# Gate and up products as 2x2 blocks, with seven block products for three of eight k-tile pairs, in a two-layer encoder trunk on one Trainium2 core

## The chip, the cores and the metric

The kernel runs on one core of one Trainium2 chip. The metric is the device time of one execution in microseconds; the times are medians of several runs. The profile is one further execution with the hardware profiler on.

A core has engines that work side by side, each with its own instruction stream: TensorE (PE in the profile, its weight loads PEld), VectorE (DVE), ScalarE (ACT), GpSimd (POOL) and SyncE (SP), which here starts the weight transfers. TensorE multiplies a stationary tile with a moving one and adds into PSUM; the other engines work from SBUF or PSUM to either.

## What is computed

```python
for layer in range(DEPTH):                       # DEPTH = 2
    h = rms_norm(x, ln_mix_g[layer])             # x: 256 tokens x 2048
    mix = even_mixer(h, ...) if layer % 2 == 0 else odd_mixer(h, ...)
    x = x + mix
    h = rms_norm(x, ln_ffn_g[layer])
    x = x + (jax.nn.silu(h @ wg) * (h @ wu)) @ wd   # wg, wu: 2048 x 5632, wd: 5632 x 2048
```

All of it is float32. Layer 0 mixes by retention and a gated spatial unit, layer 1 by a gated linear recurrence and sparse attention. The change touches the products h @ wg and h @ wu of both layers.

## The kernel before

A product in float32 is made of three matmuls: the weight and the activation are each split into a rounded part hi and a rest lo, and hi x hi, hi x lo and lo x hi are added in PSUM (lines 137 to 139 in `gemm`). The activation is stationary, 128 features by 128 tokens; the weight is the moving operand, 128 features by 512 columns. 256 tokens make two token halves, `th` 0 and 1.

Weights come by SyncE in loads of four k tiles (128 x 2048 floats, 1 MB) into `raw`, of which there are three buffers. `piece` splits 1024 columns of it: ScalarE casts to `hi` (line 93), VectorE subtracts to get `lo` (line 94); four buffers each. So a weight load feeds 24 matmuls of 512 columns.

`ffn` goes through 11 column groups of 512 hidden columns in each layer, in phases of 4, 4 and 3. For a group, the gate product goes over 16 k tiles into two PSUM banks `pg`, ScalarE takes Silu of both halves (line 259), the up product goes into two banks `pu`, and VectorE multiplies (line 263). `to_mix2` then transposes the two halves by TensorE into `pt_hid` and splits them into `hid` (lines 184, 185); it is put into the list `late`, which `gemm` empties after the first weight load of the next product. After each phase the four `pd` products multiply the phase's hidden tiles by wd and VectorE adds them to x (line 239). In the last phase `norm.feed` transposes x for the next norm's operands, `A` (lines 188, 189), `norm.finish` works out each token's factor.

PSUM has eight banks: four carry the tag "mm" (the products of `gemm`), four the tag "sm" (transposes and small products). SBUF temporaries come from one pool `temps` of 17 buffers for the whole kernel.

The order of the instructions on each engine is not the order of the code: a scheduler sets it when the program is built, by its own estimates, and each engine then works strictly in that order, waiting where an operand or a buffer isn't ready. The preparations of layer 1 (masks, a bias table `skew` made by one small product `pbias`, copied to `bt` and written to device memory by GpSimd's queue, line 448) stand in the code before the first FFN.

## Time and profile before

| | |
|---|---|
| median of 3 runs | 2262.45 us (2262.1 to 2263.41) |
| span of the profiled execution | 2260.8 us |
| TensorE busy | 2246.2 us, 99% |
| VectorE busy | 1257.9 us, 56% |
| ScalarE busy | 1013.3 us, 45% |
| device memory read | 414.29 MB, 185 GB/s over the span |
| granted TensorE clock | 0.998 |

The profiled execution's own time is its span, 2260.8 us; the median of the runs without the profiler is 1.65 us above it. A duration in the trace is that of one instruction; two that follow each other may overlap, so the distance of their starts tells more of an engine's pace than their durations. For TensorE above all the pace is read from starts: a product of 512 columns shows 0.39 us, but the next one starts long before that is over.

### The profile page before, as it was taken

The numbers are of one execution on the slowest core, as the hardware profiler recorded it, in microseconds if no ns is written. First come the engines' busy times: TensorE is split into PE (matmuls) and PEld (weight loads), VectorE is DVE, ScalarE is ACT, GpSimd is POOL, SyncE is SP. The second block draws the span as 40 slices with busy tenths as digits, with TensorE's granted clock in tenths as the row PEclk, the third lists the DMA queues.
The fourth block names the chain that finished last, engine by engine and source line by source line (L and its number), as shares of the span: only waits on it lengthen the run. The fifth ranks groups of instructions, "written<-read, shape, count | busy, mean of one in ns | idle before, by whom it ended". The sixth has DMA issues, their size and how long they took to land.

```text
span 2260.8 us, 26089 instructions
## 1 busy us (share of the span) xinstructions
PE 2246.2 (99%) x10397; PEld 1870.2 (83%) x10397; DVE 1257.9 (56%) x1763; ACT 1013.3 (45%) x1268; POOL 12.1 (1%) x24
## 2 busy tenths in 40 slices
PE   9999999999999999999999999999999999999999
PEld 7888888788888888888898888888888888888887
DVE  6645666444544455455555787865445444544554
ACT  6444445344434443444555355554443344434442
POOL 0000000000000000000000000000000000000000
PEclk9999999999999999999999999999999999999999
DMA  8555455655555555555455443355555555555553
GB/s 323 205 187 188 166 179 180 183 186 193 195 189 188 193 195 186 189 196 188 161 196 190 146 149 126 125 188 189 188 196 187 188 191 198 186 188 198 192 186 149
DMA packets 63433, 419.64 MB, mean 186 GB/s; under 512 B 7672, under 2 KB 7672, under 8 KB 15696
## 3 DMA queue, kind: packets, MB, share of 16 engines
q1 hardware_dynamic: 60704, 412.51, 51.0%
q0 software_dynamic: 1312, 3.33, 0.8%
q10 hardware_dynamic: 1296, 2.15, 0.3%
q8 instruction: 81, 1.33, 0.2%
q14 instruction: 40, 0.33, 0.0%
HBM read 414.29 MB, written 3.67 MB: 185 GB/s over the span
## 4 chain that ended last, share of the span: by engine, by line
PE 97%; DMA 1%; DVE 1%; ACT 1%; issue 0%; SPq 0%; ACTq 0%
PE pu L138 8%; PE pu L139 8%; PE pu L137 8%; PE pg L137 7%; PE pg L139 7%; PE pg L138 7%; PE pd L139 7%; PE pd L137 7%; PE pd L138 7%; PE po L139 2%; PE po L138 2%; PE po L137 2%; PE pqk L139 1%; PE pqk L138 1%; PE pqk L137 1%; PE plv L655 1%
## 5 line engine op out<-in xcount | busy, mean ns | idle before, releaser
L94 DVE TENSOR_TENSOR lo<-raw,hi 128x1024 fp32r<-128x1024 f32 (+3 forms) x784 | 948.6, 1211 | 958.2 <-ACT hi L93 957.7
L93 ACT CAST hi<-raw 128x1024 fp32r<-128x1024 f32 (+3 forms) x784 | 817.0, 1043 | 1143.0 <-PE pu L139 300.4
L137 PE MATMUL pu<-hi,A 128*128 128x512 f32 x768 | 300.4, 391 | 4.8 <-ACT hi L93 4.8
L137 PE MATMUL pg<-hi,A 128*128 128x512 f32 x768 | 300.6, 391 | 0.0
L138 PE MATMUL pu<-lo,A 128*128 128x512 f32 x768 | 299.9, 390 | 0.5 <-DVE lo L94 0.5
L139 PE MATMUL pu<-hi,A 128*128 128x512 f32 x768 | 299.8, 390 | 0.0
L139 PE MATMUL pg<-hi,A 128*128 128x512 f32 x768 | 299.0, 389 | 0.0
L138 PE MATMUL pg<-lo,A 128*128 128x512 f32 x768 | 298.8, 389 | 0.0
L137 PE MATMUL pd<-hi,hid 128*128 128x512 f32 x704 | 274.7, 390 | 0.0
L139 PE MATMUL pd<-hi,hid 128*128 128x512 f32 x704 | 274.0, 389 | 0.0
L138 PE MATMUL pd<-lo,hid 128*128 128x512 f32 x704 | 273.9, 389 | 0.0
L137 PEld LDWEIGHTS pu<-hi,A 128*128 128x128 f32 x768 | 144.8, 189 | 35.2 <-ACT hi L93 5.2
L138 PEld LDWEIGHTS pu<-lo,A 128*128 128x128 f32 x768 | 144.8, 189 | 31.1 <-DVE lo L94 1.0
L139 PEld LDWEIGHTS pu<-hi,A 128*128 128x128 f32 x768 | 144.7, 188 | 30.2
L139 PEld LDWEIGHTS pg<-hi,A 128*128 128x128 f32 x768 | 144.2, 188 | 30.1
L137 PEld LDWEIGHTS pg<-hi,A 128*128 128x128 f32 x768 | 144.2, 188 | 29.9 <-issue 0.6
L138 PEld LDWEIGHTS pg<-lo,A 128*128 128x128 f32 x768 | 144.2, 188 | 29.4
L139 PEld LDWEIGHTS pd<-hi,hid 128*128 128x128 f32 x704 | 132.1, 188 | 27.5
L138 PEld LDWEIGHTS pd<-lo,hid 128*128 128x128 f32 x704 | 132.2, 188 | 27.1
L137 PEld LDWEIGHTS pd<-hi,hid 128*128 128x128 f32 x704 | 132.2, 188 | 27.2
L137 PE MATMUL pqk<-hi,A 128*128 128x512 f32 x128 | 50.5, 394 | 0.0
L138 PE MATMUL pqk<-lo,A 128*128 128x512 f32 x128 | 49.9, 390 | 0.0
(337 smaller groups left out, 2322.4 us busy)
## 6 DMA issues: line engine op xcount, KB each, us to landing
raw<-in_wg SPq DMA_DIRECT2D x88, 1024.0 KB, 4.8
raw<-in_wu SPq DMA_DIRECT2D x88, 1024.0 KB, 4.8
raw<-in_wd SPq DMA_DIRECT2D x88, 1024.0 KB, 4.8
raw<-in_ev_in SPq DMA_DIRECT2D x44, 1024.0 KB, 4.8
raw<-in_od_in SPq DMA_DIRECT2D x32, 1024.0 KB, 4.8
raw<-in_ev_out SPq DMA_DIRECT2D x16, 1024.0 KB, 4.8
raw<-in_od_out SPq DMA_DIRECT2D x16, 1024.0 KB, 4.7
raw<-in_od_z SPq DMA_DIRECT2D x8, 720.0 KB, 4.1
```

What stands on the lines that cost most here:

```text
L93: nc.scalar.copy(hi[:, :e], raw[:, o : o + e])
L94: nc.vector.tensor_sub(lo[:, :e], raw[:, o : o + e], hi[:, :e].bitcast(F32))
L137: mm(ps[th], xh[:, c], hi[:, j, :], start=i + j == 0, stop=False)
L138: mm(ps[th], xh[:, c], lo[:, j, :], start=False, stop=False)
L139: mm(ps[th], xl[:, c], hi[:, j, :], start=False, stop=i + j == total - 1)
L655: mm(ps[:, i, th, :], lhs[:, i, t], rhs[:, i, t], start=True, stop=True)
```

## The change

Each weight load now holds two k tiles of gate and the same two of up for a column group: gate of the first, gate of the second, up of the second, up of the first (`_gate_up`, in the host's layout). `gate_up` takes the place of the two `gemm` calls of a group. The eight loads of a group are its k-tile pairs 0 to 7. A pair is a product of 2x2 blocks: two token halves by two k tiles, times two k tiles by gate and up.

Pairs 0, 2, 3, 5 and 7 do the eight block products as before, 24 matmuls, into the banks q2 (gate, half 0), q4 (gate, half 1), q3 (up, half 0) and q8 (up, half 1). Pairs 1, 4 and 6 (`MIXED`) do seven: VectorE makes four sums of weight blocks (`sum`), ScalarE and VectorE split three plain blocks (`hu`, `lu`, 1536 columns) and the four sums (`ht`, `lt`, 2048 columns), and each of the seven products goes into one of seven banks: q1, q5, q6 and q7 are of the tag "sm", q2, q3 and q4 are those of the plain pairs. After pair 6, ScalarE copies q1 and VectorE works out u2, u3, v and w from q1, q5, q6 and q7; after pair 7 these are added to q2, q4, q3 and q8, then come Silu and the product. The activation's side of the blocks is made once for each norm, by `left` for the tiles 1, 4 and 6.

The temporaries come from a pool for each stage (`m0`, `f0`, `m1`, `f1`), opened and closed around it. The preparations of layer 1 now stand in the code behind the first FFN, with the pool `m1`. GpSimd's transfer descriptors get 4096 bytes instead of the default. Comment lines are emptied.

```diff
+MIXED = (1, 4, 6)
...
+    def stage(name, bufs):
+        stack = ExitStack()
+        now["T"] = stack.enter_context(tc.tile_pool(name="T" + name, bufs=bufs))
+        return stack
...
+    def left(src, gs):
+        g, h = T([4, 128], "g"), T([4, 128], "h")
+        nc.scalar.activation(g[:, 0:4:3, :], src[:, 0, :].rearrange("p (i n) -> p i n", i=2), AF.Copy, scale=gs[0])
+        nc.scalar.activation(g[:, 1:3, :], src[:, 1, :].rearrange("p (i n) -> p i n", i=2), AF.Copy, scale=gs[1])
+        nc.vector.tensor_sub(h[:, 0, :], g[:, 3, :], g[:, 2, :])
+        nc.vector.tensor_sub(h[:, 3, :], g[:, 0, :], g[:, 3, :])
+        nc.vector.tensor_sub(h[:, 1, :], h[:, 0, :], g[:, 0, :])
+        nc.vector.tensor_add(h[:, 2, :], g[:, 1, :], h[:, 1, :])
+        out = []
+        for t, n in ((g, 3), (h, 4)):
+            a = act.tile([128, 2, 4, 128], F32R, tag="A", name="A", bufs=8 + len(MIXED))
+            nc.scalar.copy(a[:, 0, 0:n, :], t[:, 0:n, :])
+            nc.vector.tensor_sub(a[:, 1, 0:n, :], t[:, 0:n, :], a[:, 0, 0:n, :].bitcast(F32))
+            out += [(a[:, 0, i, :], a[:, 1, i, :]) for i in range(n)]
+        return out
...
+    def gate_up(w, n, fp):
+        q = {}
+        def bank(i):
+            if i not in q:
+                q[i] = (PS if i in (1, 5, 6, 7) else PM)([512], f"q{i}")
+                return q[i], True
+            return q[i], False
+        def product(i, x2, hi, lo, last=False):
+            (xh, xl), (ps, first) = x2, bank(i)
+            mm(ps, xh, hi, start=first, stop=False)
+            mm(ps, xh, lo, start=False, stop=False)
+            mm(ps, xl, hi, start=False, stop=last)
+        c = {}
+        for j in range(8):
+            raw = load(w[j], 2048)
+            end = j == 7
+            if j not in MIXED:
+                a = n.tiles[j]
+                for o, cols in ((0, ((2, 0), (4, 1))), (1024, ((3, 0), (8, 1)))):
+                    hi, lo = piece(raw, o, 2, 512)
+                    for i, th in cols:
+                        t = slice(128 * th, 128 * th + 128)
+                        for e in range(2):
+                            kt = 1 - e if o else e
+                            product(i, (a[:, kt, 0, t], a[:, kt, 1, t]), hi[:, e, :], lo[:, e, :], end and e == 1)
+            else:
+                a11, a12, a22, d1, d2, d3, d4 = n.tiles[j]
+                r = raw.rearrange("p (i n) -> p i n", i=4)
+                sm = fp.tile([128, 4, 512], F32, tag="sum", name="sum")
+                nc.vector.tensor_add(sm[:, 0:2, :], r[:, 0:3:2, :], r[:, 3:4, :].to_broadcast([128, 2, 512]))
+                nc.vector.tensor_add(sm[:, 2, :], sm[:, 0, :], r[:, 2, :])
+                nc.vector.tensor_add(sm[:, 3, :], sm[:, 2, :], r[:, 1, :])
+                parts = []
+                for src, m, name in ((r[:, 0:3, :], 3, "u"), (sm, 4, "t")):
+                    hi = fp.tile([128, m, 512], F32R, tag="h" + name, name="h" + name)
+                    lo = fp.tile([128, m, 512], F32R, tag="l" + name, name="l" + name)
+                    nc.scalar.copy(hi, src)
+                    nc.vector.tensor_sub(lo, src, hi.bitcast(F32))
+                    parts += [(hi[:, i, :], lo[:, i, :]) for i in range(m)]
+                b11, b21, b22, s1, s2, s3, s4 = parts
+                last = j == MIXED[-1]
+                product(1, a11, *b11, last)
+                product(2, a12, *b21)
+                product(3, d3, *b22)
+                product(5, d1, *s1, last)
+                product(7, d4, *s2, last)
+                product(6, d2, *s3, last)
+                product(4, a22, *s4)
+                if last:
+                    c1 = T([512], "c1")
+                    nc.scalar.copy(c1, q[1])
+                    u2, u3, v, w_ = T([512], "u2"), T([512], "u3"), T([512], "v"), T([512], "w")
+                    nc.vector.tensor_add(u2, c1, q[6])
+                    nc.vector.tensor_add(u3, u2, q[7])
+                    nc.vector.tensor_sub(v, q[5], u2)
+                    nc.vector.tensor_sub(w_, q[5], u3)
+                    c = {2: c1, 4: u3, 3: v, 8: w_}
+            if j == 0:
+                flush()
+            elif j == 1:
+                flush2()
+        for i in (2, 4, 3, 8):
+            nc.vector.tensor_add(c[i], q[i], c[i])
...
     def ffn(layer, n, norm):
+        f = stage(f"f{layer}", TF)
+        fp = f.enter_context(tc.tile_pool(name=f"sums{layer}", bufs=1))
         for g0, gn in ((0, 4), (4, 4), (8, 3)):
             hid = []
             for g in range(g0, g0 + gn):
-                pg = two(512, "pg")
-                gemm(pg, wg[g], n.get, 512, range(4))
...
-                pu = two(512, "pu")
-                gemm(pu, wu[g], n.get, 512, range(4))
...
+                late.append(partial(to_mix2, gate_up(wgu[g], n, fp), "hid", hid))
...
+    ffn(0, nf0, n1)
...
+    c1 = stage("m1", TB)
+    lp = c1.enter_context(tc.tile_pool(name="l1", bufs=1))
     masks = lp.tile([128, 7, 128], I32, name="masks")
```

The scheduler's order shows the new work at three places. First VectorE where one column group ends and the next is under way, before: two products with the up half, `s`, stand between plain splits, and the two splits of hidden tiles follow three plain splits later (`lo` and `hi` are split weights, `pu` a PSUM bank, `r` the tokens' factor).

```order
L94 TENSOR_TENSOR lo_3966<-raw_3963,hi_3965 128x1024
L263 SCALAR_TENSOR_TENSOR s0_3767<-pu0_3771,r_3067,s0_3767 128x512
L263 SCALAR_TENSOR_TENSOR s1_3768<-pu1_3772,r_3067,s1_3768 128x512
L94 TENSOR_TENSOR lo_3982<-raw_3963,hi_3981 128x1024
L94 TENSOR_TENSOR lo_4000<-raw_3997,hi_3999 128x1024
L94 TENSOR_TENSOR lo_4016<-raw_3997,hi_4015 128x1024
L185 TENSOR_TENSOR hid_3947<-pt_hid_3948,hid_3947 128x2x256
L185 TENSOR_TENSOR hid_3955<-pt_hid_3956,hid_3955 128x2x256
```

After, on VectorE at the same place, with the four additions of banks (`c1`, `u3`, `v`, `w`), and `lt`, the 2048-column split of the next group's pair 1.

```order
L350 TENSOR_TENSOR c1_3916<-q2_3657,c1_3916 128x512
L350 TENSOR_TENSOR u3_3919<-q4_3664,u3_3919 128x512
L350 TENSOR_TENSOR v_3920<-q3_3675,v_3920 128x512
L325 TENSOR_TENSOR lt_4033<-sum_4024,ht_4032 128x2048
L350 TENSOR_TENSOR w_3921<-q8_3682,w_3921 128x512
L354 SCALAR_TENSOR_TENSOR c1_3916<-v_3920,r_3069,c1_3916 128x512
L354 SCALAR_TENSOR_TENSOR u3_3919<-w_3921,r_3069,u3_3919 128x512
L104 TENSOR_TENSOR lo_4064<-raw_4061,hi_4063 128x1024
L104 TENSOR_TENSOR lo_4080<-raw_4061,hi_4079 128x1024
L104 TENSOR_TENSOR lo_4098<-raw_4095,hi_4097 128x1024
L195 TENSOR_TENSOR hid_4006<-pt_hid_4007,hid_4006 128x2x256
L195 TENSOR_TENSOR hid_4014<-pt_hid_4015,hid_4014 128x2x256
```

The splits of the hidden tiles still come three plain splits behind the last product, but ahead of these rows there now stand `lt` of pair 6, two plain splits, the three additions and `lu` of the next group's pair 1, and u2, u3, v and w. Second, TensorE behind the transposes of a hidden tile, before: products into `pg`, banks of the other tag.

```order
L178 MATMUL pt_hid_3658<-ident_80,s0_3469 128x128
L178 MATMUL pt_hid_3658<-ident_80,s1_3470 128x128
L137 MATMUL pg0_3613<-hi_3667,A_2802 128x512
L138 MATMUL pg0_3613<-lo_3668,A_2802 128x512
L139 MATMUL pg0_3613<-hi_3667,A_2802 128x512
```

These products wait for no bank that the transposes use. After, the end of the first mixed pair that follows the transposes:

```order
L296 MATMUL q5_4046<-ht_4032,A_2727 128x512
L297 MATMUL q5_4046<-lt_4033,A_2727 128x512
L298 MATMUL q5_4046<-ht_4032,A_2727 128x512
L296 MATMUL q7_4050<-ht_4032,A_2727 128x512
L297 MATMUL q7_4050<-lt_4033,A_2727 128x512
L298 MATMUL q7_4050<-ht_4032,A_2727 128x512
L296 MATMUL q6_4054<-ht_4032,A_2727 128x512
L297 MATMUL q6_4054<-lt_4033,A_2727 128x512
L298 MATMUL q6_4054<-ht_4032,A_2727 128x512
L296 MATMUL q4_3981<-ht_4032,A_2724 128x512
```

Here q7 and q6 take the banks of the two `pt_hid` tiles, and wait for the two hidden splits shown above.

Third, TensorE around the small product behind which the bias table is copied and written, before: between the first mixer's output (`po`) and the first FFN (`pg`).

```order
L138 MATMUL po1_2858<-lo_2936,mixb_2367 128x512
L139 MATMUL po1_2858<-hi_2935,mixb_2367 128x512
L445 MATMUL pbias_2966<-onehot_2961,relb_2963 8x384
L137 MATMUL pg0_2989<-hi_2993,A_2706 128x512
L138 MATMUL pg0_2989<-lo_2994,A_2706 128x512
```

After, between the end of the first FFN (`pd`) and layer 1's first products (`pz`).

```order
L148 MATMUL pd1_8007<-lo_8119,hid_7668 128x512
L149 MATMUL pd1_8007<-hi_8118,hid_7668 128x512
L555 MATMUL pbias_8154<-onehot_8149,relb_8151 8x384
L147 MATMUL pz0_8176<-hi_8180,A_7787 128x360
L148 MATMUL pz0_8176<-lo_8181,A_7787 128x360
```

The copy `bt` and the write of `skew` follow this product, and so move from the first FFN to layer 1's start.

## Rows read from the trace of the kernel before

**Rows 1.** The page's first part (busy us, share, count), then TensorE's waits.

```profile
PE 2246.2 (99%) x10397; PEld 1870.2 (83%) x10397; DVE 1257.9 (56%) x1763; ACT 1013.3 (45%) x1268; POOL 12.1 (1%) x24
...
PE pu L137 <- ACT hi L93: 4.8, 1, 4.8
```

**Rows 2.** Timeline of TensorE, two stretches (start us, us, engine, line, operation).

```profile
443.14 1.03 PE L178 MATMUL pt_hid<-ident,s 128*128 128x128 f32 x8
...
444.48 0.39 PE L139 MATMUL pg<-hi,A 128*128 128x512 f32 x1
...
513.18 0.39 PE L138 MATMUL pu<-lo,A 128*128 128x512 f32 x1
513.41 0.39 PE L139 MATMUL pu<-hi,A 128*128 128x512 f32 x1
...
521.80 0.39 PE L137 MATMUL pu<-hi,A 128*128 128x512 f32 x1
```

**Rows 3.** VectorE's groups by form (busy us, mean ns | idle), then VectorE's timeline.

```profile
L94 DVE TENSOR_TENSOR lo<-raw,hi 128x1024 fp32r<-128x1024 f32 x756 | 924.9, 1224 | 931.8 <-ACT hi L93 931.5
...
L263 DVE SCALAR_TENSOR_TENSOR s<-pu,r,s 128x512 f32<-128x512 f32 x44 | 30.9, 743 | 0.0
L185 DVE TENSOR_TENSOR hid<-pt_hid,hid 128x512 fp32r<-128x512 f32 x44 | 28.2, 682 | 0.0
...
L683 DVE TENSOR_TENSOR qp<-qp,em 128x128 f32<-128x128 f32 x48 | 13.5, 282 | 1.6 <-PE pl L670 1.5
...
L94 DVE TENSOR_TENSOR lo<-raw,hi 128x768 fp32r<-128x768 f32 x4 | 3.8, 958 | 6.9 <-ACT hi L93 6.9
...
L690 DVE TENSOR_TENSOR em<-em 128x128 f32<-128x128 f32 x4 | 1.1, 287 | 0.0
...
15.68 2.35 DVE L94 TENSOR_TENSOR lo<-raw,hi 128x1024 fp32r<-128x1024 f32 x2
...
40.93 0.16 DVE L168 SCALAR_TENSOR_TENSOR nr_y<-nr_t,nr_y 128x2 f32<-128x2 f32 x1
41.12 0.17 DVE L230 COPY r<-nr_y 128x2 f32<-128x2 f32 x1
...
371.71 1.28 DVE L239 TENSOR_TENSOR x<-po,x 128x512 f32<-128x512 f32 x2
```

**Rows 4.** ScalarE's groups by form, then the timeline where engines hand over.

```profile
L93 ACT CAST hi<-raw 128x1024 fp32r<-128x1024 f32 x756 | 796.0, 1053 | 1117.8 <-PE pu L139 300.4 <-PE pd L139 271.2 <-PE pg L139 269.1
...
L184 ACT CAST hid<-pt_hid 128x512 fp32r<-128x512 f32 x44 | 23.5, 586 | 0.0
...
L93 ACT CAST hi<-raw 128x768 fp32r<-128x768 f32 x4 | 3.3, 834 | 5.2 <-PE phq L139 3.8 <-issue 1.5
...
501.85 0.39 PE L139 MATMUL pg<-hi,A 128*128 128x512 f32 x1
...
502.28 1.05 ACT L93 CAST hi<-raw 128x1024 fp32r<-128x1024 f32 x1 [1.67 <-PE pg L139]
...
503.36 1.22 DVE L94 TENSOR_TENSOR lo<-raw,hi 128x1024 fp32r<-128x1024 f32 x1 [1.50 <-ACT hi L93]
```

**Rows 5.** Transfers (KB, us to landing), TensorE's timeline, one window (PEclk third from the end).

```profile
raw<-in_wu SPq DMA_DIRECT2D x88, 1024.0 KB, 4.8
...
raw<-in_od_z SPq DMA_DIRECT2D x8, 720.0 KB, 4.1
...
skew<-bt POOLq DMA_DIRECT2D x1, 1536.0 KB, 34.8
...
raw<-in_wu SPq DMA_DIRECT2D x1, 1024.0 KB, 23.8
...
417.74 0.79 PE L137 MATMUL pu<-hi,A 128*128 128x512 f32 x1 [4.75 <-ACT hi L93]
...
424.28 0.40 PE L138 MATMUL pu<-lo,A 128*128 128x512 f32 x1
...
420.00:425.00 5.00, 5.00 (x15) 3.87 (x14) 3.59 (x3) 4.09 (x5) 0.00 (x0) 0.57 0.59 210
```

More of the change, by code (lines that the diff above doesn't have):

```diff
@@ L70, in trunk @@
     nc.scalar.activation(warm, warm, AF.Gelu)
-    idle = tp.tile([128, 512], F32R, tag="T", name="idle")
+    c0 = stage("m0", TB)
+    idle = T([512], "idle", F32R)
     nc.gpsimd.memset(idle.bitcast(F32), 0.0)
@@ L209, in operand @@
         def operand(self, i, src):
-            a = act.tile([128, 2, 2, S], F32R, tag="A", name="A")
-            split(a, src, [gain(self.g0 + 2 * i), gain(self.g0 + 2 * i + 1)])
+            gs = [gain(self.g0 + 2 * i), gain(self.g0 + 2 * i + 1)]
+            if i in self.mixed:
+                self.tiles.append(left(src, gs))
+                return
+            a = act.tile([128, 2, 2, S], F32R, tag="A", name="A", bufs=8 + len(MIXED))
+            split(a, src, gs)
             self.tiles.append(a)
@@ L248, in out_proj @@
                     late.append(partial(norm.feed, c))
+    def gate_up(w, n, fp):
[61 more added lines that the diff above has]
+            nc.vector.tensor_add(c[i], q[i], c[i])
+        s = []
+        for th, (g, u) in enumerate(((2, 3), (4, 8))):
+            nc.scalar.activation(c[g], c[g], AF.Silu, scale=n.tok(th))
+            nc.vector.scalar_tensor_tensor(c[g], c[u], n.tok(th), c[g], op0=OP.mult, op1=OP.mult)
+            s.append(c[g])
+        return s
@@ new lines, in load_ln @@
+    def load_ln(q):
+        for at, t, src in ((1, lng, "sgu_g"), (4, lnb, "sgu_b")):
+            if q == at:
+                nc.sync.dma_start(t, d[src].rearrange("(o c n) -> o c n", o=1, c=2).to_broadcast([128, 2, 512]))
+    vs = [[None, None], [None, None]]
+    vps = []
+    for c in range(2):
+        ps = two(512, "pvs")
+        gemm(ps, win[10 + c], n0.get, 512, range(4), before=load_x if c else first_norm, quick=c == 0)
+        vps.append(ps)
+    nc.sync.dma_start(wsT, d["sgu_wT"])
@@ new lines, in trunk @@
+    nc.sync.dma_start(rot, d["rot"])
+    nc.sync.dma_start(dm, d["decay"])
+    v, sg = [[None, None], [None, None]], [[None, None], [None, None]]
+    for c in range(2):
+        ps = two(512, "pv")
+        gemm(ps, win[4 + c], n0.get, 512, range(4))
+        for th in range(2):
+            v[th][c] = T([512], "v")
+            nc.scalar.activation(v[th][c], ps[th], AF.Copy, scale=n0.tok(th))
+    for c in range(2):
+        ps = two(512, "pg0")
+        gemm(ps, win[6 + c], n0.get, 512, range(4))
+        for th in range(2):
+            sg[th][c] = T([512], "sg")
+            nc.scalar.activation(sg[th][c], ps[th], AF.Silu, scale=n0.tok(th))
@@ new lines, in trunk, with rotate @@
+    cs = lp.tile([128, 2, 2, 128], F32, name="cs")
+    sc = lp.tile([128, 2, 2, 128], F32, name="sc")
+    for th in range(2):
+        nc.vector.tensor_scalar(cs[:, th], rot[:, th], n0.tok(th), None, op0=OP.mult)
+        for i in range(2):
+            nc.vector.tensor_copy(sc[:, th, i, :], cs[:, th, 1 - i, :])
+    mixb = []
+    def rotate(rr, ts):
+        for i in range(2):
+            pt = turn([r[:, 256 * i : 256 * i + 256] for r in rr], "pqkT")
+            t = T([2, S], "qkT")
+            nc.scalar.copy(t, pt)
+            ts.append(t)
@@ L803, in _wide, with _gate_up @@
     return np.ascontiguousarray(w).reshape(c // n, k // (128 * dk), 128, dk * n)
+def _gate_up(g, u):
+    g, u = (w.reshape(8, 2, 128, -1, 512).transpose(3, 0, 2, 1, 4) for w in (g, u))
+    return np.ascontiguousarray(np.stack([g[:, :, :, 0], g[:, :, :, 1], u[:, :, :, 1], u[:, :, :, 0]], 3)).reshape(-1, 8, 128, 2048)
 def _cols(v):
```

262 lines of the change are left out of this document (109 added, 153 removed).

## The prediction

> **What bounds the kernel now.** I read the busy shares of the page first: the reader is to see that TensorE is busy for 2246.2 of 2260.8 us, while VectorE and ScalarE are busy for 56% and 45% [rows 1]. Then the waits of TensorE: outside the start, the only one of weight is 4.8 us, once, for a split of weights in the first FFN [rows 1]. So almost every microsecond is a product that follows the one before. The timeline of one column group gives their pace: products start at 513.18, 513.41, ... 521.80 us, 38 steps in 8.62 us, 0.2267 us each [rows 2]. The eight transposes of a finished hidden tile and two products take 443.14 to 444.48 us, so the transposes cost 1.34 - 2 x 0.2267 = 0.89 us [rows 2]. A column group of gate and up is 2 x 16 k tiles x 2 token halves x 3 = 192 products: 43.5 us, with its transposes 44.4 us. The kernel has 22 of them, 43% of its time.
>
> **What is taken away.** Five k-tile pairs keep 24 products (120), three have seven block products of three matmuls each (63): 183 instead of 192. The order shows 9584 TensorE rows against 9782: 198 = 22 x 9 fewer. All stood on the path, so 198 x 0.2267 = 44.9 us go, if TensorE stays the bound. The weights moved are the same: eight loads of 1 MB per group.
> The pace is a row, and a page can be set beside it. The Trainium skill, "TensorE: Matmul & The Clock Gate", section "Back-to-back issue gap", gives N / 2.4 + 2.5 ns, about 216 ns for 512 columns: an estimate of 42.7 us by it. The trace shows 227 ns here.
>
> **What VectorE gets instead.** Durations and starting distances are two things. One split of 128x1024 takes 1.224 us, but two that wait for nothing take 2.35 us together, so the second starts 1.13 us after the first; two additions of 128x512 (0.682 us) take 1.28, a distance of 0.60. One that needs the result of the one before starts only after its end: 40.93, then 41.12, for 0.16 us [rows 3]. From 128x768 (0.958) to 128x1024 (1.224) a column costs 1.04 ns, which makes 1.76 us for 1536 and 2.29 us for 2048 columns, distances 1.67 and 2.20 [rows 3]. A mixed pair costs VectorE three additions (1.13 + 0.71 + 0.60) and two splits (1.67 + 2.20): 6.3 us, where TensorE needs 21 x 0.2267 = 4.8 us for it. A group: ten plain splits 11.3, three mixed pairs 19.0, four combinations of banks 2.5, four additions of banks 2.4, two products with the up half 1.3, two splits of hidden tiles 1.2: 37.7 us, against 20.6 before and 42.4 us that TensorE now needs (183 x 0.2267 + 0.89). VectorE is at 89% in these stretches, but still the smaller. No row shows the additions on weights; that they cost what other fp32 additions cost I take from the rows nearest to them, on tiles with strides and a repeated operand, where 128x128 takes 0.282 us against 0.287 without [rows 3]. ScalarE: ten casts of 1.053 [rows 4], three of 1.49 and three of 1.93 (by the same slope, 0.834 to 1.053), one copy, two Silu, two hidden casts: 24 us of 42.4, hidden.
>
> **Where VectorE's order can hold TensorE.** All eight PSUM banks are now in use inside a group: q2, q4, q3, q8 in one set of four, q1, q5, q7, q6 in the other, which the transposes pt_hid share. By the order, q7 and q6 of the first mixed pair of a group wait until the two hidden splits of the group before have read pt_hid. These two stand on VectorE behind a long row: the 2048 columns of the last mixed pair, the preparation of the next group's first mixed pair, the combinations and additions of the banks, and three plain splits. I follow it from E, the end of the products of pair 4. ScalarE sees an end 0.2 us late (501.85 + 0.39, cast at 502.28, minus the 0.227 of a step) and hands on in 0.03 us [rows 4], so its 2048-column cast (1.93) lets VectorE start at E + 2.16. The row up to the hidden splits sums, by distances, to 2.20 + 3 x 1.13 + 0.71 + 0.60 + 1.67 + 0.71 + 6 x 0.60 + 2.20 + 0.60 + 2 x 0.66 + 3 x 1.13 = 20.4: it reaches them at E + 22.6. Their ScalarE casts end at E + 22.9: TensorE comes to the transposes at E + 5.44 + 4.76 + 5.44 + 5.44 = E + 21.08, ScalarE first does a cast that waits for the same point (1.05), then 0.59. So the banks are free at E + 23.6 and E + 24.2; TensorE, undisturbed, begins pair 1 after the transposes, at E + 21.97, and takes q1, q2, q3, q5, q7, q6, q4 in this order, 0.68 us each: it wants q7 at E + 24.7 and q6 at E + 25.4. A margin of 1.1 us: I take this at nothing. It is the narrowest place, and lies at 16 transitions (three, three and two in each layer; after the last group of a phase the down products follow, which need neither). A raw tile adds little: the last mixed pair's buffer is free at the end of its 1536-column split, some 1.4 us before E + 2.16; the next load lands 4.8 us later [rows 5], within 0.1 us of when the next addition wants it (E + 5.5).
>
> **Smaller terms.** The first group of each layer follows a norm: two of the three mixed operands of a layer were built earlier, the third, and the 14 small steps of the norm's factor, 0.19 us apart [rows 3], stand on VectorE between the preparations of pairs 1 and 4. Laid out in the same way, the 2048-column splits come 1.1 and 0.6 us late: 2 us a layer, 4 in all, between 0 and 8.
> The 1.5 MB write of the bias table, skew, moves. Before it runs beside the start of the first FFN: it takes 34.8 us, and a weight load issued beside it 23.8 us instead of 4.8 [rows 5]. TensorE runs dry: 4.75 us idle, then from 417.74 to 424.28 us thirteen products in 6.54 us instead of 2.95, at a granted clock of 0.57 between 420 and 425 us, its lower level of 1.2 GHz for most of that [rows 5]. Together 4.75 + 3.6 = 8.3 us. This goes from the FFN. But the table's tile now comes from the pool of layer 1, opened after the FFN, and the write is issued after the one small product ahead of pz. There loads are 720 KB, 4.1 us each [rows 5], and feed TensorE for some 4 us apiece instead of 5.44, so the same loads in flight cover less. I let the loss return with 3 us on top; bounds are -8.3 (the smaller loads slip through) and +8 (a load comes after 20 us, while the three buffers hold 12 us of work). On GpSimd's queue the same four small loads and two memsets stand ahead of the write as before. For the smaller descriptor area of these transfers no row gives a price; the write is the only large one, and its bounds cover that.
> The pools by stage open where their memory was last used tens of microseconds before; the order shows no engine that waits there for the end of a stage in front of others but the casts above. Nothing, up to 2 us.
>
> **Sum**, against the profiled execution: 2260.8 - 44.9 + 4 + 3 = 2222.9 us; the median of the runs lies 1.65 us above that span, so 2224.5 us.
>
> **Rivals.** *VectorE's row ends last.* If every step waits for the end of the one before, as the dependent ones do (duration + 0.03), the row is 5 x 1.224 + 1.22 + 1.36 + 1.76 + 8 x 0.682 + 2 x 2.29 + 2 x 0.743 + 21 x 0.03 = 22.6 us instead of 20.4: the first hidden split ends at E + 25.5, and TensorE stands 0.8 us for q7. Sixteen times that is 13 us, 2237 us; with late loads on top it may be 1.5 us each, 24 us, 2249 us. It decides once the row is 1.1 us longer. For it: VectorE at 89% and in order. Against: the distances in [rows 3].
> This is also what a rule makes of it: the Trainium skill, "VectorE: DVE Perf Modes", section "Terms", says of the DRAIN after each operation that the "next op can't issue until 8-slice pipe empties". By that rule, full durations add up and 2237 us result; the trace agrees for dependent steps (0.19 us apart at 0.16 us) but not for independent ones, 0.60 apart at 0.68.
> *VectorE becomes the bound, and the kernel slower.* The additions on strided weight tiles (1.13 + 0.71 + 0.60) might run at half pace, 2.1 us more a pair, 6.4 a group: 44.1 us, as long as a group before, so no gain, about 2262; with full durations (37 steps x 0.085 = 3.1) 47.2 us, 22 x 2.8 = 62 us more than before, about 2325. It decides at 44.4 us a group, 2.2 us more for each mixed pair. Against it speak the two 128x128 rows in [rows 3].
> *The write of the table is covered* beside pz: 8.3 + 3 us less, 2213 us. For it the smaller loads, against it the 23.8 us.
>
> **How the numbers follow.** Forecast, 2215 to 2236 us: 0.62. VectorE's row last, 2236 to 2249: 0.20. Table covered and nothing else late, below 2215: 0.07. VectorE's additions dearer, gain eaten up: 0.05 within 0.2% of before and 0.06 slower (0.2% is about what a measurement of this kernel tells from no change). Range 2214 to 2248 us: the forecast, nearly all of the first rival and the edge of the third, 0.82. Faster 0.89, same 0.05, slower 0.06.
>
> **What would show it.** Products 0.2267 us apart inside mixed pairs too; 198 fewer; VectorE near 38 us per column group, 828 us in all 22 instead of 453, its 1024-column addition near 1.22 us. TensorE's waits: if the forecast holds, none for the hidden splits at q7 or q6 in pair 1 but for the first group of a layer; if the first rival, 0.8 us and more at 16 places. No gap near 410 us, one near 1100 to 1140 us beside pz. The prediction is wrong if TensorE waits inside a column group at other places (a 2048-column split of pair 4 or 6 that comes late), or if a product's pace changes with the order of the weights.

## The result, and the profile after

The changed kernel takes 2230.9 us, median of 4 runs (2228.9 to 2232.1), the kernel before 2262.3 (2262.1 to 2263.4): a ratio of 0.986, interval 0.9846 to 0.9874. It is faster by 31.4 us, where the forecast had 38. The profiled execution after spans 2229.0 us, before 2260.8.

The page's first part answers to [rows 1]:

```profile
PE 2211.7 (99%) x10199; PEld 1833.3 (82%) x10199; DVE 1613.1 (72%) x2161; ACT 1107.1 (50%) x1302; POOL 12.1 (1%) x24
```

So do TensorE's waits (engine, line, releaser: total us, times, longest); of weight are:

```profile
PE pz L147 <- ACT hi L103: 7.9, 1, 7.9
...
PE pz L148 <- DVE lo L104: 0.7, 2, 0.4
```

198 products are gone (10397 to 10199), TensorE is still the bound, and no wait stands in a column group. The wait before at L137 in the first FFN is gone, and one beside pz has come. Windows over the first FFN and over pz, of the kernel before (columns: stretch, us, then busy time and count of PE, PEld, DVE, ACT and POOL, granted clock, DMA share, GB/s):

```profile
383.30:1125.00 741.70, 736.48 (x3294) 609.31 (x3293) 374.12 (x364) 315.05 (x343) 1.08 (x1) 1.00 0.54 188
1125.00:1157.20 32.20, 32.20 (x201) 32.17 (x200) 19.07 (x36) 17.61 (x27) 0.00 (x0) 1.00 0.56 192
```

And of the changed kernel: one column group, the first FFN, pz, and five microseconds inside pz:

```profile
458.00:500.84 42.84, 42.84 (x192) 35.17 (x191) 38.19 (x38) 23.21 (x21) 0.00 (x0) 1.00 0.54 197
382.40:1097.80 715.40, 715.40 (x3192) 588.33 (x3190) 552.39 (x567) 361.89 (x357) 3.03 (x5) 1.00 0.53 193
1097.80:1142.40 44.60, 35.98 (x201) 34.96 (x201) 17.95 (x35) 16.50 (x27) 1.10 (x1) 0.89 0.66 173
1120.00:1125.00 5.00, 0.00 (x0) 0.00 (x0) 0.00 (x0) 0.00 (x0) 0.00 (x0) 0.80 0.49 103
```

The first FFN is 26.3 us shorter; pz is 12.4 us longer, and for five whole microseconds of it no engine computes while the DMA engines are half busy: the table's write takes 34.8 us, as in [rows 5]. TensorE's granted clock is 0.89 in pz, against 1.00 before. A column group takes 42.84 us, where 42.4 were reckoned. The difference is in the mixed pairs. TensorE's timeline of plain pair 3 of a group (from 527.90) and of the mixed pair 4 behind it (start us, us, engine, line, operation):

```profile
527.90 0.39 PE L296 MATMUL q<-hi,A 128*128 128x512 f32 x1
...
533.34 0.40 PE L296 MATMUL q<-hu,A 128*128 128x512 f32 x1
...
538.23 0.39 PE L296 MATMUL q<-hi,A 128*128 128x512 f32 x1
```

24 plain products take 5.44 us, 0.2267 each, as in [rows 2]; the 21 of the mixed pair take 4.89, 0.233 each (4.89 or 4.90 in the pairs 4 and 6 of that FFN; 4.97 or 4.98 in pair 1 where it stands behind the transposes). Nothing is waited for there, the granted clock is 1.00, and the first few products of the next plain pair are slow as well (5.46 us for its 24). Found here, this pace was the question for the experiments; the table's write was the other.

VectorE's prices came as reckoned (line, names, shapes, count | busy us, mean ns | idle before):

```profile
L325 DVE TENSOR_TENSOR lt<-sum,ht 128x2048 fp32r<-128x2048 f32 x66 | 151.0, 2287 | 44.9 <-ACT ht L324 44.9
L325 DVE TENSOR_TENSOR lu<-raw,hu 128x1536 fp32r<-128x1536 f32 x66 | 115.7, 1753 | 14.6 <-ACT hu L324 14.6
L317 DVE TENSOR_TENSOR sum<-raw 128x1024 f32<-128x1024 f32 x66 | 80.3, 1217 | 0.0
L319 DVE TENSOR_TENSOR sum<-sum,raw 128x512 f32<-128x512 f32 x66 | 45.5, 690 | 1.8
```

### The profile page after: what moved, and what is told of

Its sections match the earlier page's. It is cut to its first block, busy times and chain, and to the rows that moved or that the text cites. A ratio compares the mean times of both kernels' runs of the same rounds, so it can differ in the third digit from the quotient of the medians.

```text
span 2229.0 us, 26164 instructions
## 1 busy us (share of the span) xinstructions
PE 2211.7 (99%) x10199; PEld 1833.3 (82%) x10199; DVE 1613.1 (72%) x2161; ACT 1107.1 (50%) x1302; POOL 12.1 (1%) x24
## 4 chain that ended last, share of the span: by engine, by line
PE 97%; DMA 1%; DVE 1%; ACT 0%; issue 0%; SPq 0%; ACTq 0%
PE q L296 14%; PE q L297 14%; PE q L298 14%; PE pd L149 7%; PE pd L148 7%; PE pd L147 7%; PE po L149 3%; PE po L148 2%; PE po L147 2%; PE pqk L149 1%; PE pqk L148 1%; PE pqk L147 1%; PE plv L758 1%; DMA raw<-in_od_z 1%; PE pt_hid L188 1%; PE pvs L147 1%
## 5 line engine op out<-in xcount | busy, mean ns | idle before, releaser
L103 ACT CAST hi<-raw 128x1024 fp32r<-128x1024 f32 (+3 forms) x652 | 677.6, 1040 | 936.1 <-PE q L298 277.4
L104 DVE TENSOR_TENSOR lo<-raw,hi 128x1024 fp32r<-128x1024 f32 (+3 forms) x652 | 781.8, 1206 | 492.1 <-ACT hi L103 490.6
L297 PE MATMUL q<-lo,A 128*128 128x512 f32 x880 | 343.1, 390 | 0.0
L296 PE MATMUL q<-hi,A 128*128 128x512 f32 x880 | 343.1, 390 | 0.0
L298 PE MATMUL q<-hi,A 128*128 128x512 f32 x880 | 342.6, 389 | 0.0
L296 PEld LDWEIGHTS q<-hi,A 128*128 128x128 f32 x880 | 165.2, 188 | 35.3
L297 PEld LDWEIGHTS q<-lo,A 128*128 128x128 f32 x880 | 165.2, 188 | 35.3
L298 PEld LDWEIGHTS q<-hi,A 128*128 128x128 f32 x880 | 165.2, 188 | 35.0
L325 DVE TENSOR_TENSOR lt<-sum,ht 128x2048 fp32r<-128x2048 f32 x66 | 151.0, 2287 | 44.9 <-ACT ht L324 44.9
L324 ACT CAST ht<-sum 128x2048 fp32r<-128x2048 f32 x66 | 126.2, 1912 | 59.8 <-PE q L298 51.9
L325 DVE TENSOR_TENSOR lu<-raw,hu 128x1536 fp32r<-128x1536 f32 x66 | 115.7, 1753 | 14.6 <-ACT hu L324 14.6
L298 PE MATMUL q<-ht,A 128*128 128x512 f32 x264 | 104.3, 395 | 0.0
L296 PE MATMUL q<-ht,A 128*128 128x512 f32 x264 | 103.6, 395 | 0.0
L317 DVE TENSOR_TENSOR sum<-raw 128x1024 f32<-128x1024 f32 x66 | 80.3, 1217 | 0.0
```

Source lines behind the costliest of these rows:

```text
L103: nc.scalar.copy(hi[:, :e], raw[:, o : o + e])
L104: nc.vector.tensor_sub(lo[:, :e], raw[:, o : o + e], hi[:, :e].bitcast(F32))
L296: mm(ps, xh, hi, start=first, stop=False)
L297: mm(ps, xh, lo, start=False, stop=False)
L298: mm(ps, xl, hi, start=False, stop=last)
L317: nc.vector.tensor_add(sm[:, 0:2, :], r[:, 0:3:2, :], r[:, 3:4, :].to_broadcast([128, 2, 512]))
```

## The experiments

**Which operand is slow?** p1_operands puts one side of the block products back to the plain kind, in each of the three mixed pairs another; p2_quiet leaves out the sums and splits of nearly all mixed pairs, and with them that work of VectorE and ScalarE beside the products.

p1_operands:

```
+                if j == 4:                       # stationary tiles of plain pair 3
+                    a = n.tiles[3]
+                    sides = [(a[:, i % 2, 0, 128 * (i // 2) : 128 * (i // 2) + 128], ...) for i in range(4)]
+                    a11, a12, a22, d1, d2, d3, d4 = sides + sides[:3]
+                if j == 6:                       # moving tiles of plain pair 5
+                    b11, b21, b22, s1, s2, s3, s4 = [(hi5[:, i % 2, :], lo5[:, i % 2, :]) for i in range(7)]
+                if j == 1:                       # two banks instead of seven
+                    for k, (x2, w2) in enumerate(...):
+                        product((2, 4)[k % 2], x2, *w2)
```

> The changed kernel with one operand of the block products put back to the plain pairs' kind in each of the three mixed pairs, so that its numbers are not the reference's: pair 1 sums its seven products into two banks (q2 and q4 in turn) instead of seven; pair 4 takes its stationary tiles from the plain pair 3 instead of the blocks that left() made; pair 6 takes its moving tiles from the splits of the plain pair 5 instead of hu, lu, ht and lt. The sums and splits still run. In the changed kernel the 21 products of a mixed pair take 4.90 us (pairs 1 and 6) and 4.97 us (pair 4, which the transposes stand ahead of), where 21 of the plain distance 0.2267 us are 4.76 us. If the slower pace comes from the number of banks, pair 1 falls to about 4.76 and the others stay. If it comes from the stationary blocks, pair 4 falls to about 4.83. If it comes from the moving tiles' place or row length, pair 6 falls to 4.76. If it comes from the work of VectorE and ScalarE beside the products, none of them changes.

(The text on record has the transposes ahead of pair 4; they stand ahead of pair 1.) p2_quiet keeps hu to lt of a layer's first mixed pair:

```
+                if kept:
+                    parts = kept[0]
+                else:
+                    ...
+                    kept.append(parts)
```

> The changed kernel with the sums and splits of the mixed pairs made once a layer (in its first column group's first mixed pair) and used by all later mixed pairs, so that its numbers are not the reference's: 65 of 66 times VectorE's 1.22 + 0.68 + 0.69 + 1.75 + 2.29 us and ScalarE's 1.48 + 1.91 us are left out in each layer but for the first pair. Products, their operands' places and their banks stay as they are. If the work of VectorE and ScalarE beside the products slows them, the 21 products of a mixed pair take 4.76 us instead of 4.90, and the span falls by about 9 us to 2220. If it is the operands or the banks, they stay at 4.90 us, and the span stays within 2 us of 2229, since nothing of the sums was waited for.

(The text on record counts 65 of 66 pairs; by the edit it is 32 of the 33 mixed pairs of each layer.)

TensorE's timeline of p1_operands, pair 1 from 517.07, pair 4 from 532.97 and pair 6 from 543.33, which now has plain moving tiles:

```profile
517.07 0.48 PE L296 MATMUL q<-hu,A 128*128 128x512 f32 x1
...
522.04 0.39 PE L296 MATMUL q<-hi,A 128*128 128x512 f32 x1
...
532.97 0.40 PE L296 MATMUL q<-hu,A 128*128 128x512 f32 x1
537.87 0.39 PE L296 MATMUL q<-hi,A 128*128 128x512 f32 x1
...
543.33 0.39 PE L296 MATMUL q<-hi,A 128*128 128x512 f32 x1
...
548.09 0.39 PE L296 MATMUL q<-hi,A 128*128 128x512 f32 x1
```

Pair 4 keeps 4.90 us with other stationary tiles, pair 1 keeps 4.97 with two banks; pair 6 takes 4.76 for its 21 products (2228.0 us in all, one run). So it is something about the moving tiles. In p2_quiet, pair 6:

```profile
543.52 0.40 PE L296 MATMUL q<-hu,A 128*128 128x512 f32 x1
548.41 0.39 PE L296 MATMUL q<-hi,A 128*128 128x512 f32 x1
```

4.89 us still, and 2229.5 us in all (one run): neither the mixed pairs' own work on VectorE and ScalarE nor a wait for it is the cause. The plain splits still run beside the products.

**Place, shape or data?** p3_place sets plain splits high and part of the sums' splits low.

```
+                    if j == 3 and not o:     # four tiles of 512 columns in the stage's pool
+                        hl = [T([512], "tmp", F32R) for _ in range(4)]
+                    elif j == 5 and not o:   # two tiles of 1024 columns behind lt
+                        hf, lf = (fp.tile([128, 2, 512], F32R, tag=t, name=t) for t in ("hf", "lf"))
...
+                    if j == 6 and m == 4:    # the sums' splits in the plain hi and lo
+                        for o in (0, 1024):
+                            hi, lo = piece(s2, o, 2, 512)
```

> The changed kernel, its sums unchanged, with three sets of moving tiles at other places in SBUF, so that the place is told from the tiles' shape and from the data. In the changed kernel the plain pairs' splits lie at 30 to 62 KB of a partition, hu to lt at 187 to 216 KB. Here the first half of pair 3 (plain, 12 products) lies in four tiles of 512 columns at 158 to 179 KB, the first half of pair 5 (plain, 12 products) in two tiles of 1024 columns at 216 to 224 KB, and the second part of pair 6 (12 products of the sums' splits) in the plain pairs' tiles at 30 to 62 KB. If the place makes the moving tiles slow, pair 5 rises from 5.46 to about 5.54 us (12 times 0.0063 us) and pair 6 falls from 4.89 to about 4.81; pair 3 tells whether 158 to 179 KB is slow too (5.44 or 5.52). If it is the 1536 and 2048 columns of their tiles, pair 3 and 5 stay and pair 6 falls. If it is the data (sums and differences), all three stay at 5.44, 5.46 and 4.89.

Its timeline: the first half of pair 5 (hf) and the second part of pair 6 (hi):

```profile
538.79 0.39 PE L296 MATMUL q<-hf,A 128*128 128x512 f32 x1
541.59 0.39 PE L296 MATMUL q<-hi,A 128*128 128x512 f32 x1
...
546.43 0.39 PE L296 MATMUL q<-hi,A 128*128 128x512 f32 x1
549.17 0.39 PE L296 MATMUL q<-hi,A 128*128 128x512 f32 x1
```

Twelve plain products with hf take 2.80 us; twelve block products with hi take 2.74, where twelve times 0.2267 is 2.72 and the first few still lag; the first half of pair 3 took 2.79 instead of 2.72 (2232.6 us in all, one run). So neither data nor the tiles' length counts. I read this as: high in SBUF is slow. It was wrong, because two things had been moved at once: hi and lo begin at a multiple of 1024 bytes, all the tiles high up 640 bytes past one.

**The table's write.** s1_spread and b1_before_spread write it in pieces, in the changed kernel and in the one before.

```
-    nc.gpsimd.dma_start(skew, bt[0:8, None, :].to_broadcast([8, 128, 384]))
...
+                if layer == 0 and g < 8:
+                    nc.scalar.dma_start(skew[g], bt[g : g + 1, None, :].to_broadcast([1, 128, 384]))
```

> The changed kernel with the position bias table written in eight pieces of 192 KB, one head each, from ScalarE's queue at the ends of the first eight column groups of the first FFN, instead of one write of 1536 KB from GpSimd's queue beside the first layer-1 products (pz). If the 12.4 us that pz lost (1157.2 to 1142.4 us for its end against 1125.0 to 1097.8 for its start) are due to that one write, pz goes back to the 32.2 us that it took in the kernel before, and if a piece fits in the slack of the loads (4.8 us to land against 5.4 us of products on a load), the FFN loses nothing: 2230.9 - 12.4 = 2218.5 us. If the pieces hold back the loads as the whole did (8.3 us for 1536 KB in the first FFN of the kernel before), the gain is 12.4 - 8.3 = 4 us: 2227 us. If pz was late for another cause (the wait for the pools of the new stage), it stays at 2231.

> The kernel before with the same table written in the same eight pieces inside the first FFN. There the one write cost 8.3 us, the 68 products that raw loads held back: 2262.3 - 8.3 = 2254 us if the pieces fit in the slack, 2262 if they hold the loads back as the whole did. The difference of this kernel and the changed kernel with the same pieces is then the block products' own gain without the table's write: 44.9 us less what the slower pace in the mixed pairs costs (10.4 us by the profile's start distances) and what the first column groups lose (0 to 4): 31 to 35 us if the pace is the mis-sized term, 41 if the pace's excess is no real time.

Both came out slower than any time that was expected: 2238.4 us (ratio to before 0.9896, 0.9881 to 0.9911) and 2278.4 (1.0075, 1.0059 to 1.0092). The pieces were not where the code has them. Nothing but the table was needed for them, so the scheduler that orders the program put them ahead: in s1_spread they are issued from 286 to 396 us, beside layer 0's last products. The transfers there (KB each, median us to landing):

```profile
skew<-bt ACTq DMA_DIRECT2D x8, 192.0 KB, 8.8
```

Two of the issues in ScalarE's queue:

```profile
315.02 0.49 ACTq L367 DMA_DIRECT2D skew<-bt  x1
...
330.78 0.49 ACTq L367 DMA_DIRECT2D skew<-bt  x1
```

And TensorE behind these two pieces:

```profile
317.97 0.50 PE L148 MATMUL po<-lo,mixa 128*128 128x512 f32 x1 [2.54 <-DVE lo L104]
...
333.85 0.60 PE L148 MATMUL po<-lo,mixa 128*128 128x512 f32 x1 [2.66 <-DVE lo L104]
```

TensorE waits there for 2.5 us and more (until 317.97 and 333.85) for a split of weights, and it would be easy to take this for the price of a piece. The engines that make the split show another cause. ScalarE's cast of these weights and VectorE's row ahead of the first wait:

```profile
306.85 1.05 ACT L103 CAST hi<-raw 128x1024 fp32r<-128x1024 f32 x1 [3.52 <-PE po L149]
...
313.65 0.69 DVE L271 TENSOR_TENSOR x<-po,x 128x512 f32<-128x512 f32 x1 [10.08 <-PE po L149]
...
316.69 1.23 DVE L104 TENSOR_TENSOR lo<-raw,hi 128x1024 fp32r<-128x1024 f32 x1
```

And the same kind of split in the changed kernel:

```profile
312.95 1.23 DVE L104 TENSOR_TENSOR lo<-raw,hi 128x1024 fp32r<-128x1024 f32 x1 [1.50 <-ACT hi L103]
```

The weights had landed and their cast was over at 307.90. But VectorE stands idle for 10.08 us until 313.65: two additions to x, which wait for TensorE's sums, and six small steps of the norm are ahead of the split in its order. In the changed kernel the split follows its cast. Ahead of the second wait, too, VectorE is idle for such an addition (4.32 us, until 329.42) while a cast that was over at 327.27 waits for its split, until 332.58; and in the 5 us behind the issues at 286.10 and 364.64 TensorE waits for nothing. So these waits come from the order that the scheduler chose for the program with the pieces; b1_before_spread has the same row (10.09 us of idle time, the split at 316.59). The loads beside the pieces do land later (7.2 to 8.3 us in the median between 280 and 420 us, instead of 4.8), but what a piece costs by itself is not shown: the two runs did not test it. So instead of placing the write, s2_row and b2_before_row make it small: one row a head, read with a positive step and turned round on VectorE.

```
-    skew = dp.tile([8, 128, 384], F32, name="skew")
+    skew = dp.tile([8, 384], F32, name="skew")
-    nc.gpsimd.dma_start(skew, bt[0:8, None, :].to_broadcast([8, 128, 384]))
+    nc.gpsimd.dma_start(skew, bt[0:8])
-    ... offset=base.offset + 127, ap=[[383, 128], [1, 256]]))
+    ... offset=base.offset + 1, ap=[[1, 128], [1, 256]]))
-                                               bias[:, i, 256 - n : 256], op0=OP.mult, op1=OP.add)
+                                               bias[:, i, 0:n][:, ::-1], op0=OP.mult, op1=OP.add)
-    ... == bucket[None, :]).astype(f))
+    ... == bucket[None, ::-1]).astype(f))
```

> The changed kernel with the bias table written once as 8 rows of 384 (12 KB instead of 1536 KB) at the same place in the program, its columns turned round; the reads take the same 128 KB each, and VectorE reads the tile backwards. If the write's size is what delays pz, the 7.9 us wait goes and pz takes 32.2 us again instead of 44.6: 2230.9 - 12.4 = 2218.5 us, range 2216 to 2222. If pz waits for the pools of the new stage and the small loads behind them, it stays at 2231.

> The kernel before with the same small table at its own place, ahead of the first FFN. The first FFN's 8.3 us of waiting for raw loads goes: 2262.0 - 8.3 = 2253.7 us, range 2251 to 2256, if the write is its cause; 2262 if not. The changed kernel with the small table then stands against it by the block products alone: 44.9 us less 9 to 10 us of slower pace less 0 to 4 us of first groups, 31 to 36 us; the forecast's own terms (44.9 less 4) would give 41.

2218.25 us (0.9807, 0.9792 to 0.9822) and 2253.4 (0.9961, 0.9947 to 0.9975): both within 0.4 us of the main expectation. The transfer in s2_row:

```profile
skew<-bt POOLq DMA_DIRECT2D x1, 12.0 KB, 1.7
```

No wait at pz is left in its trace. The write cost 12.7 us beside pz and 8.9 beside the first FFN.

**Is it the place?** s3_low moves the activations up, so that the block tiles come down to 64 to 121 KB; q1_before_high moves the weights of the kernel before up; p4_step sets the block tiles across the middle.

```
-    act = ctx.enter_context(tc.tile_pool(name="acts", bufs=8))
+    act = ctx.enter_context(tc.tile_pool(name="acts", bufs=8, side="right"))     # s3_low
...
-    wp = ctx.enter_context(tc.tile_pool(name="weights", bufs=4))
+    wp = ctx.enter_context(tc.tile_pool(name="weights", bufs=4, side="right"))   # q1_before_high
...
+    xp = ctx.enter_context(tc.tile_pool(name="xs", bufs=4))                      # p4_step, on s3_low
+        pad = fp.tile([128, PAD], F32, name="pad")                               # PAD = 3400
```

> The changed kernel with the small bias table (12 KB) and one more edit: the pool of the activations (x, the left operands, the hidden tiles) goes to the upper end of SBUF, so that the stage's temporaries and hu, lu, ht and lt lie at 64 to 121 KB of a partition instead of 158 to 216 KB. The plain splits stay at 30 to 62 KB. If it is the place that makes the moving tiles slow, the 21 products of a mixed pair take 4.76 us instead of 4.90 (and the first pair behind them 5.44 instead of 5.46), 10.4 us in 66 pairs: 2218.25 - 10.4 = 2208 us, range 2205 to 2212. If the place does not matter, or 64 to 121 KB is as slow as 158 KB, it stays at 2218.

> The kernel before with the weights' pool at the upper end of SBUF: the raw tiles at 172 to 197 KB and the moving tiles hi and lo at 197 to 229 KB of a partition, instead of 17 to 75 KB; the rest moves down. Nothing else changes. If the place sets the pace, every product of the weights takes 0.2333 us instead of 0.2267: 382 loads of 24 products of 512 columns, 9168 times 0.0066 = 60 us, 2262.3 + 60 = 2322 us. If it is peculiar to the block products, it stays at 2262.

> The changed kernel with the small table and the blocks' tiles set across the middle of SBUF, to find where the slow part begins: hu at 122.8 to 128.9 KB (in thousands of bytes), lu at 128.9 to 135.1, ht at 135.1 to 143.3, lt at 143.3 to 151.5. Slow at 158 and above and fast at 62 and below are shown. If the slow part begins between these tiles, a mixed pair's products split into fast ones and slow ones by tile; if it begins below, all take 4.90 us a pair as in the changed kernel; if above, all take 4.76 us.

s3_low, expected at 2208, took 2264.9 us (1.0012, 1.0002 to 1.0021), p4_step 2262.2 (one run), q1_before_high 2318.0 (1.0245, 1.0228 to 1.0262). p4_step stands on the same moved activations, so all its products are slow and it does not tell what it was made for. In s3_low not the mixed pairs became fast but the plain ones slow, though their hi and lo had not moved; from 517.64, 24 products:

```profile
517.64 0.39 PE L296 MATMUL q<-hi,A 128*128 128x512 f32 x1
...
523.24 0.39 PE L296 MATMUL q<-hi,A 128*128 128x512 f32 x1
```

5.60 us instead of 5.44. What had moved was the other operand. This ends "high moving tiles are slow"; "either operand high is slow" was left, and another reading: the beginnings of the two operands. Below, the bytes past a multiple of 1024 at which the built program places the tiles (no trace shows these), and the distance of products in the traces:

| kernel, products | stationary | moving | apart, modulo 256 | us a product |
|---|---|---|---|---|
| changed, plain | 0 | 0 | 0 | 0.2267 |
| changed, mixed | 0 | 640 | 128 | 0.233 |
| s1_spread, plain | 32 | 32 | 0 | 0.2267 |
| s1_spread, mixed | 32 | 672 | 128 | 0.233 |
| s3_low, plain | 992 | 0 | 32 | 0.233 |
| s3_low, mixed | 992 | 640 | 160 | 0.234 |
| p4_step, mixed | 992 | 928 | 192 | 0.233 |
| q1_before_high | 0 | 992 | 224 | 0.233 |

s1_spread had moved everything by 32 bytes, both operands alike, and stayed fast.

**The beginnings.** s4_aligned leaves all tiles high where they are, and sets one pad of 384 bytes ahead of them; in six groups of the second FFN the tiles are used with an offset.

```
+        pad = fp.tile([128, 96], F32, name="pad")
...
+OFF = {(1, 1): 256, (1, 2): 512, (1, 3): 768, (1, 5): 128, (1, 6): 256, (1, 7): 512}
-                    hi = fp.tile([128, m, 512], F32R, tag="h" + name, name="h" + name)
+                    hi, lo = (fp.tile([128, 512 * m + 256], ...)[:, off : off + 512 * m] ... for t in "hl")
```

> The changed kernel with the small bias table, the pools where the changed kernel has them, and one pad of 384 bytes ahead of the sums' tiles, so that hu, lu, ht and lt begin at a multiple of 1024 bytes, as the left operands A (79 to 124 KB) and the plain hi and lo do; in the changed kernel they begin 640 bytes past one. They stay at 187 to 219 KB. In six column groups of the second FFN the tiles are used from 256, 512, 768, 128, 256 and 512 bytes behind their beginning (groups 1, 2, 3, 5, 6 and 7), to see which distance counts. Both readings left fit all runs so far: either one operand above some place between 157 and 158 KB is slow, or two operands whose beginnings differ by 640, 32 or 960 bytes modulo 1024 are slow (moved activations: A at 992, hi at 0; weights at the upper end: hi at 992, A at 0; the changed kernel: A at 0, hu at 640), while equal ones are fast (the spread table: both at 32). If it is the distance, mixed pairs take 4.76 us instead of 4.90 but in the groups with an offset whose distance counts: 2218.25 - 10.4 = 2208 us, up to 2.5 more if all the offsets are slow. If it is the place, all stay at 4.90: 2218.

2209.1 us (0.9766, 0.9753 to 0.9779; on s2_row's small table), the fastest of all. Its timeline: a mixed pair of the first FFN, then pair 4 of the second FFN's group 5 (offset 128) and of group 6 (offset 256):

```profile
542.47 0.39 PE L297 MATMUL q<-hu,A 128*128 128x512 f32 x1
547.23 0.39 PE L297 MATMUL q<-hi,A 128*128 128x512 f32 x1
...
1817.48 0.40 PE L297 MATMUL q<-hu,A 128*128 128x512 f32 x1
1822.37 0.39 PE L297 MATMUL q<-hi,A 128*128 128x512 f32 x1
...
1860.17 0.39 PE L297 MATMUL q<-hu,A 128*128 128x512 f32 x1
1864.93 0.39 PE L297 MATMUL q<-hi,A 128*128 128x512 f32 x1
```

4.76 us, 4.89 us, 4.76 us. All mixed pairs of the groups with 256, 512 and 768 are as fast as those with none, and only group 5 is slow. So it is neither the place nor the shape: two operands whose beginnings lie a multiple of 256 bytes apart run at 0.2267 us, the other distances tried (32, 128, 160, 192 and 224 modulo 256) at 0.233 or 0.234. Why is not shown.

One distance more lies in all these traces: layer 1 has 72 products with the stationary tile `cq`, which begins 64 bytes short of a multiple of 256, while hi and lo begin at one. The first 18 of them, in the kernel before and in s3_low (start to the start of the product behind them):

```profile
1299.17 0.39 PE L137 MATMUL puq<-hi,cq 128*128 128x512 f32 x1
...
1303.30 0.39 PE L137 MATMUL phq<-hi,A 128*128 128x512 f32 x1
```

```profile
1300.60 0.40 PE L147 MATMUL puq<-hi,cq 128*128 128x512 f32 x1
...
1304.80 0.40 PE L147 MATMUL phq<-hi,A 128*128 128x512 f32 x1
```

4.13 us, 0.229 each, against 4.20, 0.233 each, at the same distance; in p4_step it is 0.229 again. So the distance modulo 256 does not settle the pace in every case, and there are not just two paces.

**VectorE's margin.** d1_margin adds an operation to the row that frees the transposes' banks:

```
+                    ex = fp.tile([128, 4, 512], F32, name="ex")
+                    nc.vector.tensor_sub(ex, sm, hi.bitcast(F32))
```

> The changed kernel (with its large table) and one more operation on VectorE in each column group: lt's subtraction of the third mixed pair is made a second time into a tile that nobody reads, 2.29 us, right behind the first, and so in the row that frees the two banks of the transposes. The forecast gave this row a margin of 1.1 us at q7 and at q6, and the trace of the changed kernel shows it (first split ends at 476.26 us, q7's products begin at 477.4; the second at 476.9, q6's at 478.1). If the forecast's row is right, TensorE waits 2.26 - 1.1 to 1.2 us, about 1.1, at the 16 steps from one group to the next: 2230.9 + 18 = 2249 us. If the row has slack that the forecast did not see, 2231; if it had none, 16 times 2.26 = 36: 2267.

2230.2 us (0.986, 0.9845 to 0.9874): nothing lost. But it did not test what it meant to: the program's order answered. VectorE and TensorE at one transition, of the changed kernel:

```profile
475.62 1.29 DVE L195 TENSOR_TENSOR hid<-pt_hid,hid 128x512 fp32r<-128x512 f32 x2 [0.20 <-ACT hid L194]
...
477.47 0.40 PE L296 MATMUL q<-ht,A 128*128 128x512 f32 x1
...
478.18 0.39 PE L296 MATMUL q<-ht,A 128*128 128x512 f32 x1
```

And of d1_margin:

```profile
476.85 1.28 DVE L195 TENSOR_TENSOR hid<-pt_hid,hid 128x512 fp32r<-128x512 f32 x2
...
478.09 0.40 PE L296 MATMUL q<-ht,A 128*128 128x512 f32 x1
...
478.80 0.39 PE L296 MATMUL q<-ht,A 128*128 128x512 f32 x1
```

In the changed kernel the first split ends at 476.30 and q7's products begin at 477.47: 1.17 us, and 1.27 at q6 (476.91 to 478.18). In d1_margin three plain splits of weights stand behind the hidden ones, where the changed kernel has three ahead and one behind, and TensorE takes two products of q4 ahead of q7. The margin is 0.56 us at q7 (477.53 to 478.09) and 0.67 at q6: smaller by 0.6, not by 2.3. What a late row costs here stays untested.

## Why the prediction was right, and where its sum was off

That it gets faster is right (the interval of the ratio lies clear of 1), and 2230.9 us lies inside the range of 2214 to 2248; the point is 6.4 us too low. The runs give the terms, the first groups' only as what is left.

- **Products taken away.** 198 x 0.2267 = 44.9 us. s4_aligned against b2_before_row, both with the small table, is 2253.4 - 2209.1 = 44.3 us, and one group of it still ran slow (4.98 + 4.90 + 4.90 us in its three mixed pairs instead of 4.86 + 4.76 + 4.76: 0.4 us). Right. The estimate of 42.7 us set beside it goes by a formula that the Trainium skill, "TensorE: Matmul & The Clock Gate", section "Back-to-back issue gap", gives for a single matmul by itself; for a sustained stream of 512 columns the same section states about 131 ns, an estimate of 26 us. The runs bear out neither, but the row.
- **Pace in the mixed pairs: the step that failed.** The sum took 0.2267 us for every product that is left, since before every product had it. The change put hu to lt behind tiles whose sizes sum to 640 bytes past a multiple of 1024, and the 1386 products of mixed pairs ran at 0.233, the first few behind each pair slow as well. s2_row against s4_aligned: 2218.25 - 2209.1 = 9.2 us, 9.6 with the slow group. The first sign that the text gave, products 0.2267 us apart inside mixed pairs too, did not come. It named a product's pace that changes as what would make it wrong, but guessed at the weights' order and gave it no price. The hidden assumption was that the place of a tile is free.
- **The table's write beside pz.** 3 us net were taken, between -8.3 and +8. It cost 12.7 us there (2230.9 - 2218.25) and 8.9 before (2262.3 - 2253.4): 3.8 us net. Right, and the rival that the write is covered is out.
- **First groups of a layer, and the pools.** 4 us, up to 2 more for the pools. What is left of the difference: -31.4 + 44.9 - 9.6 - 3.8 = 0.1 us. Nothing that these runs can tell: oversized. No wait in a first group shows in TensorE's list.
- **VectorE's row.** The chain from E gave margins of 1.1 and 1.2 us; the trace shows 1.17 and 1.27. VectorE was reckoned at 37.7 us a group, and is busy for 38.19 of 42.84. The rival with full durations needed the row 1.1 us longer; the distances held, and with them the row. The other one, dearer additions, is out by their rows (1217 and 690 ns).

So a term of 9.6 us was missing and one of 4 us was too many. The second hid part of the first, and that is luck: without it the point would have been some 10 us too low. Put in, they give 2224.5 + 9.6 + 0.8 - 3.9 = 2231.0; since the last term is what was left, this sum closes by construction.

## What to carry to other kernels

A new tile is not only a price on the engine that fills it: on TensorE its beginning, seen from the other operand's, set the pace of each product by 3%, and a pool of odd size ahead of it is enough to shift it. So compare the start distances of products by tile name after any change of the pools, and align pools, not tiles one by one. A large write is best made small; moving it moved the loss with it here. And where a scheduler orders the program, look at where the instruction went, and at what else changed its place, before putting a price on it.

## What the runs showed of the hardware that was not expected

- TensorE: 128x128 by 512 columns in this kernel's format, 0.2267 us apart when the stationary and the moving tile begin a multiple of 256 bytes apart, 0.233 or 0.234 when 32, 128, 160, 192 or 224 bytes off that; 64 bytes off, 0.229 in the kernel before and 0.233 in s3_low. Moving only the weights' pool of the kernel before costs 55 us of 2262.6 (q1_before_high). The Trainium skill, "SBUF — State Buffer", section "Operand start alignment", asks for a start at a multiple of the element's size and says that this is about legality, not speed; here the speed hangs on more.
- The first few products behind such a run, with well placed operands, are slow as well (5.46 or 5.47 us for most plain pairs behind a mixed one, 5.44 else).
- The table's write of 1536 KB in one transfer took 34.8 us and cost TensorE 12.7 us beside pz and 8.9 beside the first FFN; as 12 KB it landed after 1.7 us, and no wait at pz was left. Eight pieces of 192 KB landed after 8.8 us in the median, and the kernels with them are 20 and 25 us longer than those with the small table (2238.4 - 2218.25 and 2278.4 - 2253.4); the longest waits in them come from VectorE's order, and the pieces' own share is not shown.
